# Sample gathers put ahead of the gate tables, and second-stage matmuls with activations as weights and 512 moving columns

## The chip, the cores and the metric

One core of one Trainium2 chip runs the whole step; the other cores are idle. The metric is device time in microseconds (us) of one execution. Below, PE is TensorE, DVE is VectorE, ACT is ScalarE, POOL is GpSimd, SP is the queue that issues the plain transfers.

## The reference

One layer of a hybrid decoder on two groups of tokens: a prompt of 512 tokens (four tiles of 128, with 16 learned tokens in front) and 32 sample tokens. The first half (projection, RWKV-7 recurrence, windowed attention, output projection) is not touched. The second half is the retrieval of experts:

```
h = rmsnorm(x, norm2_g)
q = h @ w_query;  s = q . sub_keys                  # 8 heads, two halves of 128 keys
idx, gate = top 16 of the sums of the top 16 of each half, softmax   # 128 experts per token
pre = einsum('td,tkd->tk', h, expert_u[idx])
act = gelu(pre) * gate
x   = x + einsum('tk,tkd->td', act, expert_v[idx]);   y = rmsnorm(x)
```

expert_u and expert_v have 16384 rows of 1024 numbers each (64 MB each).

## The kernel before, in words

The kernel serves the experts in two ways.

**By gathers** (prompt tiles 0 and 3, and the samples): `experts` fetches, for each of the k chosen experts, one row per token with an indirect transfer of 128 x 1024 numbers (512 KB), issued by POOL into one of six buffers `gat`. First all u rows (DVE multiplies each with h and sums it into a column of `pre`; the page calls this CUSTOM_DVE_ANT_0), then gelu and gate, then all v rows (DVE adds each, scaled, to the output `x`: SCALAR_TENSOR_TENSOR). A tile takes 128 + 128 gathers. The samples take 32 + 32, with the 32 tokens spread four times over the partitions, and end in three small transfers that fold the four parts, three adds and an rmsnorm.

**Densely** (prompt tiles 1 and 2, 256 tokens): all 16384 experts are computed for all tokens, in 128 blocks of 128 experts. `block_in` loads u and v of a block (one `uv` buffer, 1 MB), transposes u on PE, and splits u and v into two parts each whose sum is the value (uH, uL, vH, vL; the names ending in H and L are fp32r, TensorE's faster float format). ACT makes the H parts, DVE makes uL, POOL makes vL. `block_u` makes 24 matmuls of 256 columns, gelu on ACT, two multiplications by the gates and the split into aH, aL. `block_v` makes the second product and accumulates it over all 128 blocks in four PSUM banks `acc`.

The gates of the dense blocks are a table of experts by tokens. Function `gates`, run once for tile 1 and once for tile 2, builds it in 16 steps of 8 tokens each: a one-hot `o0` on DVE (written to a buffer called uH), a second one (buffer uL), six scalings on ACT, eight matmuls, copies out of PSUM. Between the steps run pieces of `late()`, the output projection and query scores of tile 3. The top-16 search of tile 3 (`late_heads`) runs beside the first dense blocks, and tile 3's gathers beside the others.

**What sets the order.** Gathers stand in a list `side` of generators. `beside(n)` takes n steps (one gather each) from the list and emits them at that place; `tc.issue_after(mark)` lets the scheduler put them as early as the marked DVE instruction. The scheduler then orders each engine's instructions by its own model of time; engines run their instructions in that order. Before the gates, `for n in range(AHEAD)` emits 280 steps: all of tile 0 and the first of the samples. Each of the 32 gate steps calls `beside(RATE_G)` with 0.8. Each dense block calls it with 1.6 while `late_heads` runs and with 2.4 afterwards. What is left comes at the end (`beside(1000)`).

The places to follow: the loop over AHEAD (L1619), `gates` with L1448, `block_v` (L1517 to L1524), the dense loop (L1645 to L1654) and the end (L1655 to L1671).

Of the kernel before, what the change touches and what calls it, by code (L numbers as in the profile page):

```python
# [11 lines left out]
F32 = mybir.dt.float32  # L12
# [3 lines left out]
OP = mybir.AluOpType  # L16
# [16 lines left out]
LAG = 2  # L33
WST = 3
UV = 5
AHEAD = 280
RATE_G = 0.8
RATE_D = 2.4
RATE_H = 1.6
LATE = 2  # L40
# [69 lines left out]
def bc(ap, shape):  # L110
    return ap.to_broadcast(shape)
# [3 lines left out]
def hymba_step(ctx, tc, x_prompt, x_sample, cache_k, cache_v, state_wkv, state_shift, meta, norm1_g, w_in, mu, w0,  # L115
# [3 lines left out]
    A, G, T, DM = nc.scalar, nc.gpsimd, nc.tensor, nc.sync  # L119
    marks = []  # L120
# [10 lines left out]
    V = V()  # L131
    uid = [0]

    def _t(pool, tag, bufs, shape, dt=F32):
        uid[0] += 1
        return pool.tile(list(shape), dt, tag=tag, name=f"{tag}_{uid[0]}", bufs=bufs)
# [30 lines left out]
    ident = p0.tile([128, 128], F32, name="ident")  # L167
# [77 lines left out]
    side, due = [], [0.0]  # L245

    def beside(n):

        due[0] += n
        while side and due[0] >= 1.0:  # L250
            due[0] -= 1.0
            if next(side[0], None) is None:
                side.pop(0)
        due[0] = min(due[0], 1.0)
# [845 lines left out]
    def finish(x2, y, rows, dst, gf, kind="F"):  # L1100

        rms(x2[:rows], y[:rows], rows, gf, kind)
        DM.dma_start(dst, y[:rows])

    def final_g(t):
        G.dma_start(t, fin_g.partition_broadcast(128))
        return t
# [96 lines left out]
    with ExitStack() as px:  # L1204
# [36 lines left out]
        def transposed(h, half, rows):  # L1241
            p = jps().rearrange("p (a b) -> p a b", a=4)
            for j in range(4):
                k = 4 * half + j
                transpose(p[:, j, 0:rows], h[:rows, k * 128:(k + 1) * 128])
            return p

        def put(src, dst):

            A.copy(dst[0], src)  # L1250
            V.tensor_tensor(dst[1], src, dst[0].bitcast(F32), OP.subtract)
# [25 lines left out]
        for half in range(2):  # L1277
            p = transposed(hS, half, 72)
# [144 lines left out]
    def gates(its, sel, ps, put):  # L1423


        i1T, i2T, gaT = sel
        its, iot = its
        ib = dt_("aH", 2, [128, 2, 128], BF16)
        for c, x in enumerate((i1T, i2T)):
            A.copy(ib[:, c], x)  # L1430
        for n, t8 in enumerate(range(0, 128, 8)):
            ob = dt_("uL", 2, [128, 128, GA], BF16)
            o0, o1 = dt_("uH", 2, [128, 8, 128]), dt_("vH", 2, [128, 8, 128])
            V.tensor_tensor(o0.rearrange("p t j -> p j t"), its, bc(ib[:, 0, t8:t8 + 8].unsqueeze(1), [128, 128, 8]), OP.is_equal)
            V.tensor_tensor(ob, its[:, :, 0:GA], bc(ib[:, 1, t8:t8 + GA].unsqueeze(1), [128, 128, GA]), OP.is_equal)
            for q0 in (0, 4):
                p = ps()
                for q in range(q0, q0 + 4):
                    t = slice(t8 + q, t8 + q + 1)
                    if q < GA:  # L1440
                        A.mul(o1[:, q, :], ob[:, :, q], gaT[:, t])
                    else:
                        V.tensor_scalar(o1[:, q, :], iot, i2T[:, t], gaT[:, t], OP.is_equal, OP.mult)
                    T.matmul(p[:, 128 * (q - q0):128 * (q - q0) + 128], o0[:, q, :], o1[:, q, :], start=True, stop=True)  # L1444
                put(t8 + q0, p)
            if n % LATE:
                next(more, None)
            with tc.issue_after(marks[-1]):  # L1448
                beside(RATE_G)


    ND = 256
    dn = ctx.enter_context(tc.tile_pool(name="dn", bufs=1, reuse_waits="tile"))
    dp = ctx.enter_context(tc.tile_pool(name="dp", bufs=1, space=PSUM, reuse_waits="tile"))

    def dt_(tag, bufs, shape, dt=F32):
        return _t(dn, tag, bufs, shape, dt)

    def dps():
        return _t(dp, "w", 4, [128, 512])  # L1460
# [3 lines left out]
    for i in range(2):  # L1464
        hn = dt_("uv", UV, [128, 2, D])[:, 0]
        DM.dma_start(hn, hscr[1 + i])
        for half in range(2):
            p = dps().rearrange("p (a b) -> p a b", a=4)
            for j in range(4):
                k = 4 * half + j  # L1470
                T.transpose(p[:, j, :], hn[:, 128 * k:128 * k + 128], ident)
            o = hH[:, 4 * half:4 * half + 4, 128 * i:128 * i + 128]
            A.copy(o, p)
            V.tensor_tensor(hL[:, 4 * half:4 * half + 4, 128 * i:128 * i + 128], p, o.bitcast(F32), OP.subtract)

    acc = [dp.tile([128, 2, ND], F32, name=f"acc{c}", bufs=1) for c in range(4)]
    euv = eu[0].rearrange("(i j) d -> i j d", j=128)
    evv = ev[0].rearrange("(i j) d -> i j d", j=128)

# [36 lines left out]

    def block_v(j, x):  # L1517
        vH, vL, aH, aL = x
        for d in range(8):
            o = acc[d // 2][:, d % 2, :]  # L1520
            ds_ = slice(128 * d, 128 * d + 128)
            T.matmul(o, vH[:, ds_], aH, start=(j == 0 and d % 2 == 0), stop=False, skip_group_check=True)  # L1522
            T.matmul(o, vH[:, ds_], aL, start=False, stop=False, skip_group_check=True)  # L1523
            T.matmul(o, vL[:, ds_], aH, start=False, stop=(j == 127), skip_group_check=True)  # L1524

    gA, gB = dt_("gA", 1, [128, 32, 128]), dn.tile([128, 64, 128], F32, name="gB")
    sg = [None]
# [88 lines left out]
            yield True  # L1616
        coming[0] = False

    for n in range(AHEAD):  # L1619
        with tc.issue_after(marks[gather_mark[0]]):  # L1620
            beside(1)
    more = late()
    its = one_hot_table()
    sels = [sel_transposed(0, dps, dt_("selT", 1, [128, 3, 128])), sel_transposed(1, dps, dt_("lsc", 1, [128, 3, 128]))]
    gates(its, sels[0], dps, stage)
    gates(its, sels[1], dps, keep)
    for _ in more:
        pass
# [15 lines left out]
    for j in range(128):  # L1644
        nxt, mark = None, last  # L1645
        if j < 127:
            nxt, last = block_u(ins.pop(j + 1), gate_of(j + 1))
        if j < 126:
            ins[j + 2], sub = block_in(j + 2)
        block_v(j, mid)  # L1650
        mid = nxt
        next(more, None)
        with tc.issue_after(mark), tc.issue_after(sub):
            beside(RATE_H if coming[0] else RATE_D)  # L1654
    oT = gB[:, 0:16, :].rearrange("p a b -> p (a b)").rearrange("p (a b) -> p a b", b=ND)  # L1655
    for c in range(4):
        A.copy(oT[:, 2 * c:2 * c + 2, :], acc[c])
    gfd = final_g(dt_("uv", UV, [128, 2, D])[:, 0])
    for i in range(2):
        xy = dt_("uv", UV, [128, 2, D])  # L1660
        x2, y = xy[:, 0], xy[:, 1]
        DM.dma_start(x2, xscr[1 + i])
        for half in range(2):
            p = dps()
            for q in range(4):
                k = 4 * half + q
                T.transpose(p[:, 128 * q:128 * q + 128], oT[:, k, 128 * i:128 * i + 128], ident)
            xs_ = x2[:, 512 * half:512 * half + 512]
            V.tensor_tensor(xs_, xs_, p, OP.add)
        finish(x2, y, 128, y_p[0, 128 * (i + 1):128 * (i + 1) + 128, :], gfd, "E")  # L1670
    beside(1000)  # L1671

# [27 lines left out]
```

## Time and profile before

| what | value |
|---|---|
| median of 3 runs | 2180.15 us (2161.02, 2180.15, 2190.67) |
| the profiled execution | 2171.7 us |
| its span, first to last instruction | 2169.9 us |
| mean granted TensorE clock | 0.866 of full speed |
| PE busy, DVE busy, POOL busy, ACT busy | 84%, 76%, 59%, 40% of the span |
| mean transfer rate | 263 GB/s |

All places in time below are us from the span's start. The busy shares are means over stages with different limits; what matters is read per stage. The gate tables begin at 1115.7 and end at 1247.2, the dense blocks run until about 2125.

### The profile page before, as it was taken

How to read it: one execution, taken by the hardware profiler on the slowest of the kernel's cores; microseconds unless marked ns; L12 is line 12 of the kernel's file. 1: busy time of each engine (PE TensorE's matmuls, PEld its weight loads, DVE VectorE, ACT ScalarE, POOL GpSimd, SP SyncE). 2: the span in 40 equal slices, each digit the busy share in tenths (PEclk: the TensorE clock that was granted, in tenths of full speed). 3: DMA queues.
4: the chain of work that ended last, by engine and by line, in shares of the span. 5: the costliest groups of instructions: out<-in, count | busy, mean ns of one | idle time of the engine just before them, and what ended most of it. 6: DMA issues, size and time to landing. Idle time of an engine off the chain costs nothing.

```text
span 2169.9 us, 37101 instructions
## 1 busy us (share of the span) xinstructions
PE 1816.4 (84%) x13915; PEld 1693.1 (78%) x13915; DVE 1639.2 (76%) x3285; ACT 862.6 (40%) x1975; POOL 1271.9 (59%) x951
## 2 busy tenths in 40 slices
PE   5999984585685868898567998999999999999992
PEld 5888973373574757798457988899999999999992
DVE  5643426679878988678989999867676767899988
ACT  6553421221132322433258943444444444444442
POOL 0110103678777677533824365768776777888885
PEclk9999986555675768799769999999999999999996
DMA  7532373487779789966859985789999998999987
GB/s 222 164 107 81 106 199 108 156 304 237 262 247 308 242 282 323 299 222 206 271 182 330 341 287 191 287 297 392 336 336 336 330 338 330 326 322 328 328 312 261
DMA packets 311306, 571.60 MB, mean 263 GB/s; under 512 B 32916, under 2 KB 194694, under 8 KB 310983
## 3 DMA queue, kind: packets, MB, share of 16 engines
q0 software_dynamic: 84048, 305.70, 39.6%
q1 hardware_dynamic: 227078, 263.53, 37.5%
q8 instruction: 110, 1.80, 0.3%
q14 instruction: 70, 0.57, 0.1%
HBM read 544.12 MB, written 25.65 MB: 263 GB/s over the span
## 4 chain that ended last, share of the span: by engine, by line
PE 56%; DVE 17%; issue 9%; DMA 8%; POOL 7%; ACT 3%; SPq 0%; POOLq 0%; DVEq 0%; ACTq 0%
PE acc L1523 5%; PE acc L1524 5%; PE acc L1522 5%; PE w L1508 5%; PE w L1505 5%; PE w L1506 5%; PE w L1491 4%; POOL gat L1075 4%; PE pD L220 3%; DVE x L127 3%; PE pD L966 2%; DVE gat L127 2%; DMA wst<-in_w_query_dram 2%; PE ps L220 2%; PE w L1444 2%
## 5 line engine op out<-in xcount | busy, mean ns | idle before, releaser
L127 DVE SCALAR_TENSOR_TENSOR x<-gat,act,x 128x1024 f32<-128x1024 f32 x287 | 440.5, 1535 | 12.5 <-DMA gat<-in_expert_v_dram,ei 9.4
L1075 POOL DMA_INDIRECT gat<-in_expert_u_dram,ei x256 | 337.0, 1316 | 132.2 <-DVE pre L127 45.8
L1075 POOL DMA_INDIRECT gat<-in_expert_v_dram,ei x256 | 317.7, 1241 | 122.6 <-issue 35.4
L1498 POOL TENSOR_TENSOR vL<-uv,vH 128x1024 fp32r<-128x1024 f32 x128 | 335.2, 2619 | 84.0 <-ACT vH L1497 82.7
L1522 PE MATMUL acc<-aH,vH 128*128 128x256 f32 x1024 | 292.2, 294 | 6.2 <-ACT aH L1514 6.2
L1523 PE MATMUL acc<-aL,vH 128*128 128x256 f32 x1024 | 289.5, 285 | 7.0 <-DVE aL L127 6.8
L1524 PE MATMUL acc<-aH,vL 128*128 128x256 f32 x1024 | 288.6, 284 | 0.0
L1505 PE MATMUL w<-dhH,uH 128*128 128x256 f32 x1024 | 251.6, 283 | 2.7 <-DVE uL L127 1.5
L1506 PE MATMUL w<-dhL,uH 128*128 128x256 f32 x1024 | 251.3, 283 | 0.0
L127 DVE CUSTOM_DVE_ANT_0 gat<-gat,h 128x1024 f32<-128x1024 f32 x160 | 202.7, 1279 | 44.7 <-DMA gat<-in_expert_u_dram,ei 41.7
L1523 PEld LDWEIGHTS acc<-aL,vH 128*128 128x128 f32 x1024 | 197.2, 193 | 8.9 <-DVE aL L127 8.8
L1505 PEld LDWEIGHTS w<-dhH,uH 128*128 128x128 f32 x1024 | 196.7, 192 | 3.1 <-DVE uL L127 1.7
L1522 PEld LDWEIGHTS acc<-aH,vH 128*128 128x128 f32 x1024 | 192.7, 192 | 7.1 <-ACT aH L1514 7.1
L1524 PEld LDWEIGHTS acc<-aH,vL 128*128 128x128 f32 x1024 | 197.1, 192 | 0.0
L1506 PEld LDWEIGHTS w<-dhL,uH 128*128 128x128 f32 x1024 | 196.7, 192 | 0.0
L1497 ACT CAST vH<-uv 128x1024 fp32r<-128x1024 f32 x128 | 134.9, 1054 | 148.9 <-issue 111.3
L127 DVE TENSOR_TENSOR uL<-w,uH 128x512 fp32r<-128x512 f32 x256 | 166.7, 682 | 10.1 <-ACT uH L1493 10.1
L127 DVE TENSOR_TENSOR w<-w,gl 128x128 f32<-128x128 f32 x128 | 50.3, 393 | 148.6 <-ACT w L1509 148.6
L127 DVE CUSTOM_DVE_ANT_0 gat<-gat,lx 128x1024 f32<-128x1024 f32 x128 | 158.1, 1268 | 0.0
L1508 PE MATMUL w<-dhH,uL 128*128 128x256 f32 x1024 | 148.1, 286 | 4.7 <-DVE uL L127 4.3
L1493 ACT CAST uH<-w 128x512 fp32r<-128x512 f32 x256 | 138.0, 593 | 8.0
L1508 PEld LDWEIGHTS w<-dhH,uL 128*128 128x128 f32 x1024 | 133.0, 192 | 7.6 <-DVE uL L127 6.9
(568 smaller groups left out, 4046.5 us busy)
## 6 DMA issues: line engine op xcount, KB each, us to landing
uv<-in_expert_u_dram SPq DMA_DIRECT2D x128, 512.0 KB, 4.5
uv<-in_expert_v_dram SPq DMA_DIRECT2D x128, 512.0 KB, 6.0
wst<-in_w_query_dram SPq DMA_DIRECT2D x48, 512.0 KB, 6.6
wst<-in_w_out_dram SPq DMA_DIRECT2D x24, 512.0 KB
wst<-in_w_in_dram SPq DMA_DIRECT2D x20, 512.0 KB, 4.4
h2T<-in_w_in_dram SPq DMA_DIRECT2D x20, 512.0 KB, 4.2
gscr<-uv SPq DMA_DIRECT2D x10, 1024.0 KB, 5.9
uv<-in_w_query_dram SPq DMA_DIRECT2D x8, 1024.0 KB, 12.2
```

The costliest lines, as they stand in the source:

```text
L127: r = getattr(nc.vector, name)(*args, **kw)
L220: T.matmul(p[:, 0:n], w[:, k, :], x, start=(k == 0 and x is H and w is wH), stop=(k == 7 and w is wL))
L1075: G.indirect_dma_start(out=r, out_offset=None, in_=w[0], in_offset=bass.IndirectOffsetOnAxis(ap=ei[:, k:k + 1], axis=0))
L1493: A.copy(uH[:, ks, :], p)
L1497: A.copy(vH, vn)
L1498: G.tensor_tensor(vL, vn, vH.bitcast(F32), OP.subtract)
L1505: T.matmul(pre, uH[:, k, :], hH[:, k, :], start=(k == 0), stop=False)
L1506: T.matmul(pre, uH[:, k, :], hL[:, k, :], start=False, stop=False)
L1508: T.matmul(pre, uL[:, k, :], hH[:, k, :], start=False, stop=(k == 7))
L1522: T.matmul(o, vH[:, ds_], aH, start=(j == 0 and d % 2 == 0), stop=False, skip_group_check=True)
L1523: T.matmul(o, vH[:, ds_], aL, start=False, stop=False, skip_group_check=True)
L1524: T.matmul(o, vL[:, ds_], aH, start=False, stop=(j == 127), skip_group_check=True)
```

## The change

Two edits.

The loop over AHEAD becomes `while side:`, so all gathers of tile 0 and all 64 of the samples, with the samples' final norm, are emitted before the gates. The call of `beside` inside `gates` goes. The dense loop is as it was; its `beside` finds an empty list until tile 3's gathers are appended.

`block_v` changes its operands. Before, each block of 128 columns of v was the weight and 256 token columns of a moved past it: 24 matmuls of 256 columns, with outputs of model dimension by token. Now a block of 128 tokens of a is the weight and 512 columns of v move past: 12 matmuls of 512 columns, with outputs of token by model dimension. The four PSUM banks are now plain 128 x 512, and at the end the copies to `oT` and 16 transposes go, since the sums already stand the right way round.

```diff
-AHEAD = 280
-RATE_G = 0.8
...
             if n % LATE:
                 next(more, None)
-            with tc.issue_after(marks[-1]):
-                beside(RATE_G)
...
-    acc = [dp.tile([128, 2, ND], F32, name=f"acc{c}", bufs=1) for c in range(4)]
+    acc = [dp.tile([128, 512], F32, name=f"acc{c}", bufs=1) for c in range(4)]
...
         vH, vL, aH, aL = x
-        for d in range(8):
-            o = acc[d // 2][:, d % 2, :]
-            ds_ = slice(128 * d, 128 * d + 128)
-            T.matmul(o, vH[:, ds_], aH, start=(j == 0 and d % 2 == 0), stop=False, skip_group_check=True)
-            T.matmul(o, vH[:, ds_], aL, start=False, stop=False, skip_group_check=True)
-            T.matmul(o, vL[:, ds_], aH, start=False, stop=(j == 127), skip_group_check=True)
+        for n, (a, v) in enumerate(((aH, vH), (aH, vL), (aL, vH))):
+            for i in range(2):
+                for c in range(2):
+                    T.matmul(acc[2 * i + c], a[:, 128 * i:128 * i + 128], v[:, 512 * c:512 * c + 512],
+                             start=(j == 0 and n == 0), stop=(j == 127 and n == 2))
...
-    for n in range(AHEAD):
+    while side:
         with tc.issue_after(marks[gather_mark[0]]):
             beside(1)
...
-    oT = gB[:, 0:16, :].rearrange("p a b -> p (a b)").rearrange("p (a b) -> p a b", b=ND)
-    for c in range(4):
-        A.copy(oT[:, 2 * c:2 * c + 2, :], acc[c])
...
-            p = dps()
-            for q in range(4):
-                k = 4 * half + q
-                T.transpose(p[:, 128 * q:128 * q + 128], oT[:, k, 128 * i:128 * i + 128], ident)
             xs_ = x2[:, 512 * half:512 * half + 512]
-            V.tensor_tensor(xs_, xs_, p, OP.add)
+            V.tensor_tensor(xs_, xs_, acc[2 * i + half], OP.add)
```

How this moves instructions, at three places. First DVE, from the end of tile 2's top-16 search (dsel, ce) over the preparation of the dense part (dhL) to the first one-hot of the gate tables (the first uH). Before:

```order
L127 TENSOR_REDUCE dsel_16_111<-ce_7163 128x32
L127 TENSOR_TENSOR ce_7167<-iota_87,hl_7152 128x512
L127 TENSOR_REDUCE dsel_17_112<-ce_7167 128x32
L127 TENSOR_TENSOR ce_7171<-iota_87,hl_7152 128x512
L127 TENSOR_REDUCE dsel_17_112<-ce_7171 128x32
L127 TENSOR_TENSOR dhL<-w_7873,dhH 128x4x128
L127 TENSOR_TENSOR dhL<-w_7896,dhH 128x4x128
L127 TENSOR_SCALAR vH_8792<-aL_8771,selT_8775 128x128 x2
L127 TENSOR_TENSOR uH_8791<-vL_8773,aH_8787 128x128x8
```

With the change (x_1953 is the samples' output, to which a v gather is added):

```order
L125 TENSOR_REDUCE dsel_16_111<-ce_7163 128x32
L125 SCALAR_TENSOR_TENSOR x_1953_8803<-gat_8829,act_8800,x_1953_8803 128x1024
L125 TENSOR_TENSOR ce_7167<-iota_87,hl_7152 128x512
L125 SCALAR_TENSOR_TENSOR x_1953_8803<-gat_8832,act_8800,x_1953_8803 128x1024
L125 SCALAR_TENSOR_TENSOR x_1953_8803<-gat_8835,act_8800,x_1953_8803 128x1024
L125 TENSOR_REDUCE dsel_17_112<-ce_7167 128x32
L125 SCALAR_TENSOR_TENSOR x_1953_8803<-gat_8838,act_8800,x_1953_8803 128x1024
L125 TENSOR_TENSOR ce_7171<-iota_87,hl_7152 128x512
L125 SCALAR_TENSOR_TENSOR x_1953_8803<-gat_8841,act_8800,x_1953_8803 128x1024
L125 TENSOR_TENSOR dhL<-w_7873,dhH 128x4x128
L125 SCALAR_TENSOR_TENSOR x_1953_8803<-gat_8865,act_8800,x_1953_8803 128x1024
L125 TENSOR_TENSOR uH_8949<-vL_8931,aH_8945 128x128x8
```

In all, 21 of the samples' 32 u gathers stood ahead of the first uH and 11 between the gate steps; all 32 stand ahead now. Of the 32 v gathers 14 stood between gate steps and 18 in the dense part; now 22 stand ahead of the first uH and 10 between the first six gate steps. The order of every engine up to the 21st u gather is unchanged.

Second POOL, at the beginning of the dense part (vL is the dense split, eis the samples' indices, leq of tile 3's search). Before:

```order
L1498 TENSOR_TENSOR vL_10394<-uv_10374,vH_10393 128x1024
L1075 DMA gat_10619<-in_expert_v_dram,eis_102 128x1024
L1075 DMA gat_10711<-in_expert_v_dram,eis_102 128x1024
L1498 TENSOR_TENSOR vL_10494<-uv_10474,vH_10493 128x1024
L1075 DMA gat_10714<-in_expert_v_dram,eis_102 128x1024
L1075 DMA gat_10811<-in_expert_v_dram,eis_102 128x1024
L1053 TENSOR_TENSOR leq_11000<-leq_11000,ld_2334_10910 128x512
L1498 TENSOR_TENSOR vL_10579<-uv_10559,vH_10578 128x1024
```

With the change:

```order
L1073 DMA gat_8895<-in_expert_v_dram,eis_102 128x1024
L1124 DMA gat_8903<-x_1953_8803 32x1024
L1104 DMA gat_8913<-in_final_norm_g_dram 128x1024
L1132 DMA x_3149_15637<-xscr 128x1024
L1494 TENSOR_TENSOR vL_10168<-uv_10148,vH_10167 128x1024
L1012 TENSOR_TENSOR lcand_10455<-lvals_10300 128x2x16 x2
L1494 TENSOR_TENSOR vL_10191<-uv_10171,vH_10190 128x1024
```

Twelve of the samples' gathers stood between the first ten vL; none does now. Tile 3's search is spread over the first 12 dense blocks where it was spread over 17, and its gathers are used from the same block on (the 15th), two per block in the mean, as before. After the last aL, DVE has 24 v gathers left where it had 22.

Third PE, one dense block. Before (24 such matmuls):

```order
L1491 MATMUL w_14718<-ident,uv_14706 128x128 x4
L1522 MATMUL acc_7903<-aH_14614,vH_14552 128x256
L1523 MATMUL acc_7903<-aL_14615,vH_14552 128x256
L1524 MATMUL acc_7903<-aH_14614,vL_14553 128x256
L1522 MATMUL acc_7904<-aH_14614,vH_14552 128x256
```

With the change (12 such matmuls; the order of u matmuls, transposes and v matmuls within a block is the same):

```order
L1487 MATMUL w_16728<-ident,uv_16716 128x128 x4
L1518 MATMUL acc_7903<-vH_16586,aH_16636 128x512
L1518 MATMUL acc_7904<-vH_16586,aH_16636 128x512
L1518 MATMUL acc_7903<-vL_16587,aH_16636 128x512
L1518 MATMUL acc_7903<-vH_16586,aL_16637 128x512
```

## Rows read from the trace of the kernel before

**Rows 1.** The page: busy time of each engine.

```profile
PE 1816.4 (84%) x13915; PEld 1693.1 (78%) x13915; DVE 1639.2 (76%) x3285; ACT 862.6 (40%) x1975; POOL 1271.9 (59%) x951
```

**Rows 2.** Busy time of each engine by stretch; columns are named in the first line.

```profile
core 0: us, PE busy (x) PEld busy (x) DVE busy (x) ACT busy (x) POOL busy (x), PEclk, DMA share, GB/s
1021.10:1084.80 63.70, 34.94 (x253) 31.75 (x251) 60.03 (x183) 15.63 (x46) 54.13 (x52) 0.83 0.87 275
1084.80:1115.70 30.90, 15.82 (x62) 11.92 (x62) 25.57 (x122) 9.71 (x26) 9.89 (x15) 0.50 0.67 212
1115.70:1176.80 61.10, 44.27 (x283) 41.16 (x283) 54.74 (x87) 50.22 (x127) 22.11 (x12) 0.87 0.81 266
1176.80:1247.20 70.40, 69.86 (x594) 67.59 (x593) 65.85 (x84) 66.86 (x238) 26.70 (x14) 1.00 0.96 332
1255.00:1400.40 145.40, 130.57 (x1034) 126.21 (x1033) 141.08 (x356) 60.41 (x111) 91.18 (x72) 0.96 0.70 246
1400.40:1884.00 483.60, 483.60 (x4093) 483.60 (x4092) 341.63 (x637) 205.17 (x367) 358.65 (x224) 1.00 0.91 337
1884.00:2118.00 234.00, 233.56 (x1960) 232.46 (x1959) 216.78 (x250) 96.68 (x175) 199.86 (x111) 1.00 0.91 320
2118.00:2169.90 51.90, 9.25 (x63) 8.51 (x61) 41.67 (x39) 12.07 (x31) 27.84 (x23) 0.63 0.74 264
```

**Rows 3.** The chain that ended last, 1087 to 1109: start, us, what.

```profile
1087.65 2.09 DVE idxu L127 x8
...
1107.33 1.28 POOL ce L1053
```

**Rows 4.** Timeline of POOL: first and 27th of the samples' u gathers.

```profile
1021.16 1.03 POOL L1075 DMA_INDIRECT gat<-in_expert_u_dram,eis  x1 [1.61 <-DVE eis L127]
...
1087.09 0.98 POOL L1075 DMA_INDIRECT gat<-in_expert_u_dram,eis  x1 [0.16 <-DVE sD L127]
```

**Rows 5.** DVE's groups, 1021 to 1084.8: count, busy and mean ns, idle before.

```profile
L127 DVE CUSTOM_DVE_ANT_0 gat<-gat,h 128x1024 f32<-128x1024 f32 x21 | 31.7, 1515 | 2.7 <-DMA gat<-in_expert_u_dram,eis 2.7
```

**Rows 6.** DVE's groups in the gate tables, 1115.7 to 1247.2.

```profile
L127 DVE SCALAR_TENSOR_TENSOR x<-gat,act,x 128x1024 f32<-128x1024 f32 x13 | 16.7, 1281 | 0.0
L127 DVE CUSTOM_DVE_ANT_0 gat<-gat,h 128x1024 f32<-128x1024 f32 x11 | 13.3, 1214 | 0.0
...
L127 DVE TENSOR_TENSOR act<-act,gas 128x32 f32<-128x32 f32 x1 | 0.2, 191 | 2.2 <-ACT act L1089 2.2
```

**Rows 7.** DVE's groups in the first dense blocks, 1255 to 1400.4.

```profile
L127 DVE SCALAR_TENSOR_TENSOR x<-gat,act,x 128x1024 f32<-128x1024 f32 x18 | 35.3, 1964 | 0.0
...
L127 DVE CUSTOM_DVE_ANT_0 gat<-gat,lx 128x1024 f32<-128x1024 f32 x7 | 11.7, 1705 | 0.0
...
L127 DVE TENSOR_TENSOR h<-h,gat 32x1024 f32<-32x1024 f32 x3 | 4.8, 1584 | 0.4 <-DMA gat<-x 0.4
```

**Rows 8.** Timeline of ACT: gelu of the 1st, 20th and 21st dense block.

```profile
1254.96 0.37 ACT L1509 ACTIVATE w<-w 128x256 f32<-128x256 f32 x1 [2.48 <-PE w L1508]
...
1400.43 0.37 ACT L1509 ACTIVATE w<-w 128x256 f32<-128x256 f32 x1 [1.91 <-PE w L1508]
...
1407.05 0.37 ACT L1509 ACTIVATE w<-w 128x256 f32<-128x256 f32 x1 [1.91 <-PE w L1508]
```

**Rows 9.** Timeline of PE: merged runs, start, us to the last one's end, count.

```profile
252.77 3.67 PE L220 MATMUL pD<-gat,wst 128*128 128x314 f32 x24
...
1125.99 3.62 PE L1574 MATMUL w<-uv,ly 128*128 128x256 f32 x16
...
1606.45 0.28 PE L1523 MATMUL acc<-aL,vH 128*128 128x256 f32 x1
...
1609.08 0.28 PE L1524 MATMUL acc<-aH,vL 128*128 128x256 f32 x1
```

**Rows 10.** Timeline of DVE within a late dense block: two v gathers of tile 3.

```profile
1935.68 4.61 DVE L127 SCALAR_TENSOR_TENSOR x<-gat,act,x 128x1024 f32<-128x1024 f32 x2
```

**Rows 11.** DVE's groups at the end, 2125 to 2165.

```profile
L127 DVE SCALAR_TENSOR_TENSOR x<-gat,act,x 128x1024 f32<-128x1024 f32 x23 | 29.5, 1283 | 2.5 <-DMA gat<-in_expert_v_dram,ei 2.1
```

## The prediction, put on record before the changed kernel was timed

> **What bounds the kernel now.** I read the page's busy times first [rows 1]: no engine fills the span, PE is nearest. So the question is put to stages, with the table of busy time by stretch [rows 2], and there the limit changes three times. From 1021.1 to 1084.8 DVE is busy 60.0 of 63.7 us, and in the next 30.9 us 25.6; the chain there runs along DVE and, in short handshakes, POOL [rows 3]. In the gate tables (1115.7 to 1247.2) DVE has 120.6 of 131.5 us, ACT 117.1, PE 114.1: all three nearly full, PE fullest in the second half (69.9 of 70.4). In the first dense blocks (1255 to 1400.4) DVE is full (141.1 of 145.4) and PE is not (130.6). From 1400.4 to 1884 PE has no idle time at all and DVE 71%; one block takes 1407.05 - 1400.43 = 6.62 us, by the gelus [rows 8]. From 1884 on DVE is at 93% beside a full PE, and the last 51.9 us belong to leftover gathers on DVE, with PE nearly done.
>
> So the moved gathers leave two stretches that are full on several engines for one that is full on DVE alone, and the shorter matmul stream pays only where PE sets the pace.
>
> **The sum**, against the profiled execution's own 2171.7 us.
>
> 1. *The front, +42 us.* The order is unchanged up to the 21st u gather, about 1084.8. From there to the first one-hot, 33 gathers are new on DVE: 11 u and 22 v. Nearest prices: 1.21 us for a u gather and 1.28 for a v gather in the gates [rows 6], 1.28 for v at the end [rows 11], 1.52 for u in the stretch just before [rows 5]. At 11 x 1.21 + 22 x 1.28 they are 42 us, at 1.52 each they are 50. Idle DVE time to fill is 30.9 - 25.6 = 5.3 us [rows 2], handshakes with POOL of the kind that the chain shows [rows 3]. So 37 at the least, 45 at the most by DVE's work; I take 42. Transfers agree: 33 x 0.52 MB is 17 MB, with the 6.5 MB that the stretch moves now 24 MB, which at the 332 GB/s of the second gate half [rows 2] is 72 us, against 30.9 + 42 = 73. The issues on POOL have room (9.9 us busy of 30.9). The upper end is the pace seen just before: 27 gathers issued in 1087.09 - 1021.16 us [rows 4], 2.54 us each with the other work of that stretch in it; 33 x 2.54 = 84, which is +53 over the 30.9. Nothing else runs that could cover this: PE is at half clock (0.50) and half idle there already, so its clock loses nothing more either.
>
> 2. *The gates, -3 us.* DVE loses 11 u and 14 v gathers, and the 2.2 us wait on the samples' gelu [rows 6], and gets 10 v gathers and the samples' three adds and norm, all in the first six steps: about 33 us off, 17 on. But the first steps stay at DVE's pace, and the second half is at PE's. At best the stage falls to ACT's 117 us, that is -14; at worst the ten gathers lengthen the first steps by as much as the rest gains, 0.
>
> 3. *The first 19 dense blocks, -14 us.* They take 145.4 us, 19.6 more than 19 x 6.62. DVE's 18 v gathers of the samples took 35.3 us there (1.96 each, slowed), the three adds of the fold 4.8 [rows 7]; without them DVE has 101 us of work, and on POOL twelve gathers no longer stand between the vL splits. Against this, tile 3's search is packed into 12 blocks where it had 17. Its DVE work: a block's own is 341.6 / 73 - 2 x 1.21 = 2.3 us by the steady stretch [rows 2, 6], 43 in 19 blocks; with 11.7 for tile 3's first gathers [rows 7] some 46 of the 101 are search. In 12 blocks that is 46 + 12 x 2.3 = 73 us against 12 x 6.5 = 78: nearly full, with handshakes besides. I leave 8 us of the excess and count the shorter matmuls (19 x 0.13). Bounds: -5 (DVE still sets all 12 blocks) and -22.
>
> 4. *The 512-column matmul, -9 us, where PE sets the pace.* No fp32r matmul of 512 columns is in the trace. At 256 columns the step from one to the next is (1609.08 - 1606.45) / 22 = 119.5 ns; at 314 columns (3.67 - 0.31) / 23 = 146.1 ns [rows 9], where 0.31 is the duration of the last one. Per column that is 0.467 and 0.465 ns: by proportion 512 columns take 239 ns and nothing is won. The other end is a stream of 512 array cycles with the smallest overhead in the trace: the plain-float matmuls of 256 columns, at two cycles a column of the 2.4 GHz clock, follow each other at (3.62 - 0.38) / 15 = 216 ns [rows 9]. The two fp32r points lie about 13 and 15 ns over columns / 2.4 GHz, so I take a cost per matmul of 13 to 15 ns, and 228 ns. A block then takes 12 x 228 = 2.74 us for its v part, where it took 24 x 119.5 = 2.87: 0.13 us less. From 1400.4 to 1884, with PE never idle, there are 73 blocks: -9. At the bounds 0 and 73 x 0.28 = -20.
>
> The Trainium skill speaks against a gain: its page "TensorE: Matmul & The Clock Gate", section "LDWEIGHTS (loading the stationary operand)", has a load cost columns / 1.2 ns, 107 ns for 128 columns, which a 256-column stream already covers, so that halving the number of loads frees nothing. The page's "Back-to-back issue gap" has the isolated step at N / 2.4 + 2.5 ns, an estimate of 109 ns at 256 columns and 216 at 512; the trace has 119.5 at 256, so it does not hold here as it stands. By it the term would be as in the first rival below.
>
> 5. *The last 35 blocks, -2 us.* Two v gathers take 4.61 us of DVE in such a block, slowed from 1.28 each [rows 6, 10], and DVE is at 93% over the whole stretch [rows 2]: 6.49 us is less than DVE's work in many of these blocks. Bounds 0 and 35 x 0.13 = -5.
>
> 6. *The end, +2 us.* It is bound by the gathers: 24 instead of 22 after the last aL, 2 x 1.28 [rows 11]. The four copies on ACT and 16 transposes on PE that go were beside these gathers, so they give nothing; were the gathers not there, they would give 2 to 3 us.
>
> Sum: 42 - 3 - 14 - 9 - 2 + 2 = +16, that is 2171.7 + 16 = 2188 us. The profiled execution is 8 us below the median of the three runs, 2180.15, so against the median this is +0.4%. Two per cent, about what a measurement of this kernel can tell from no change, is 43.6 us: 2136.5 to 2223.8.
>
> **Rivals.**
>
> *Thin overhead.* The 512-column matmul steps at 216 ns. For: the 256-column plain-float row [rows 9] shows a step that close to its stream. Against: both fp32r points are 13 to 15 ns over theirs. Terms 3 and 4 gain another 2 and 11 us: 2175. Chance 0.17. This is the time that the page's issue-gap rule would give as well.
>
> *The front runs at the gathers' old pace (slower).* The front stretches by 53 because each gather goes through issue, transfer, DVE and the release of one of six buffers at 2.54 us [rows 4], while the search's handshakes hold POOL. For: that is the pace measured in the stretch just before, with POOL busy 54 of 63.7 us [rows 2]. Against: DVE was the full engine there and waited only 2.7 us for a transfer [rows 5], and it had (60.0 - 31.7) / 21 = 1.35 us of other work per gather, against 25.6 / 33 = 0.78 now. 2171.7 + 53 - 26 = 2199. It is slower by over 2% once the front grows by 78, that is from a pace of (78 + 30.9) / 33 = 3.3 us on; if the gathers lay wholly behind the search at 2.54, +84, the time would be 2230. Chance 0.21, of which 0.08 for more than 78.
>
> *DVE was the only brake.* The gates fall to ACT's 117 us and the first blocks to PE's, 42 - 14 - 22 - 9 - 2 + 2 = -3: 2169. For: DVE is the busiest engine in both. Against: in the second gate half PE is at 99%. Chance 0.15.
>
> *The change does not move what it says.* Excluded: the new order shows the gathers moved and 12 matmuls per block.
>
> **How the numbers follow.** The forecast has 0.45, the rivals 0.17, 0.21 and 0.15, and 0.02 is left for none of these. The likeliest case gives 2188. The range goes from the two favourable rivals together, 2169 - 13 = 2156, to the pace rival and half the spread of the runs shown above it (2199 + 15), with a few us more on each side for what varies between runs: 2152 to 2220. The favourable rivals together still stand 20 us above 2136.5, so faster by over 2%: 0.05. Slower by over 2%: 0.08 from the pace rival and 0.03 of chance in the runs, 0.11. Within 2%: 0.84.
>
> **What would show each step.** Front: the first uH about 42 us after 1115.7, near 1158, with DVE busy all the way and PE nearly idle. Gates: 125 to 130 us from first uH to last gate matmul. First dense blocks: gelu 1 to gelu 20 in about 131 us. PE: steps of 226 to 231 ns between the acc matmuls, blocks of 6.49 us. Last blocks: DVE nearly full, blocks still near 6.6. End: about 54 us from the last gelu. I am wrong on the main term if the first uH comes before 1148 or after 1170, and on the matmul if the step is under 220 or over 236 ns.

## The result, and the profile after

The changed kernel takes 2192.5 us (median of 20 runs, 2180.8 to 2200.1), the kernel before 2168.2 (20 runs, 2159.2 to 2190.7). The ratio is 1.0104, with a 95% interval of 1.0086 to 1.0121: slower by 1%, within two per cent. The forecast was 2188 us, +0.7% on its own profiled execution.

The page after, and its busy time by stretch (columns as in [rows 2]):

```profile
PE 1812.6 (83%) x12363; PEld 1628.4 (74%) x12363; DVE 1676.1 (76%) x3285; ACT 862.5 (39%) x1972; POOL 1276.0 (58%) x951
```

```profile
1080.90:1149.50 68.60, 15.55 (x62) 12.06 (x62) 65.23 (x168) 13.71 (x31) 56.95 (x48) 0.50 0.93 328
1149.50:1180.00 30.50, 22.19 (x121) 20.63 (x122) 30.43 (x38) 18.56 (x47) 11.15 (x8) 0.74 0.85 257
1180.00:1227.40 47.40, 34.90 (x227) 32.95 (x227) 35.37 (x50) 38.12 (x99) 1.49 (x3) 0.82 0.70 209
1227.40:1290.80 63.40, 62.85 (x530) 60.54 (x530) 44.73 (x62) 60.32 (x221) 0.00 (x0) 1.00 0.69 229
1302.30:1425.60 123.30, 120.58 (x818) 110.90 (x818) 94.12 (x293) 57.42 (x102) 69.29 (x54) 1.00 0.60 218
1425.60:1901.50 475.90, 475.79 (x3214) 438.81 (x3213) 386.49 (x635) 203.71 (x366) 378.50 (x222) 1.00 0.93 338
1901.50:2133.60 232.10, 231.01 (x1541) 211.30 (x1540) 221.91 (x249) 97.44 (x175) 197.39 (x108) 1.00 0.90 320
2133.60:2191.00 57.40, 7.89 (x24) 5.64 (x23) 44.87 (x42) 9.73 (x27) 31.60 (x26) 0.57 0.76 265
```

The page hardly moved: PE lost 3.8 us of busy time, DVE gained 36.9. The stretches moved a lot. In the front DVE is busy 65.2 of 68.6 us with PE at half clock and mostly idle; the second gate half lost 14.8 us of DVE work and did not get a microsecond shorter, since PE fills it (its row before stands next); the first dense blocks are now PE's.

```profile
1183.90:1247.20 63.30, 62.76 (x530) 60.49 (x530) 59.49 (x75) 60.25 (x221) 24.35 (x13) 1.00 0.97 336
```

To place the microseconds I use marks that both traces have: the first sample gather on POOL [rows 4], the first one-hot uH, the 17th (the first of tile 2), the last gate matmul, and the 1st, 20th and last gelu [rows 8]. After, by the timelines of POOL, DVE and ACT:

```profile
1018.00 1.04 POOL L1073 DMA_INDIRECT gat<-in_expert_u_dram,eis  x1 [1.62 <-DVE eis L125]
```

```profile
1149.54 3.62 DVE L125 TENSOR_TENSOR uH<-vL,aH 128x1024 f32<-128x1024 bf16 x2
```

```profile
1302.33 0.37 ACT L1505 ACTIVATE w<-w 128x256 f32<-128x256 f32 x1 [4.18 <-PE w L1504]
...
1425.60 0.37 ACT L1505 ACTIVATE w<-w 128x256 f32<-128x256 f32 x1 [1.78 <-PE w L1504]
...
1432.09 0.37 ACT L1505 ACTIVATE w<-w 128x256 f32<-128x256 f32 x1 [1.78 <-PE w L1504]
...
2133.63 0.37 ACT L1505 ACTIVATE w<-w 128x256 f32<-128x256 f32 x1 [0.35 <-PE w L1504]
```

The first sample gather itself, ahead of everything that was changed, came anywhere from 1012.6 to 1032.1 us in the traces of this study, so the stretches are counted from it. For every kernel of the study (us):

| kernel | front | gates 1 | gates 2 | to 1st gelu | first 19 blocks | other blocks | end | sum |
|---|---|---|---|---|---|---|---|---|
| before | 94.6 | 68.2 | 63.3 | 7.8 | 145.5 | 717.6 | 51.8 | 1148.7 |
| the change | 131.5 | 77.9 | 63.3 | 11.6 | 123.3 | 708.0 | 57.4 | 1173.0 |
| gathers_only | 130.5 | 76.7 | 63.2 | 10.7 | 125.8 | 718.0 | 52.1 | 1177.0 |
| block_v_only | 94.3 | 70.3 | 63.4 | 7.8 | 144.9 | 708.0 | 58.4 | 1147.1 |
| narrow_256 | 130.5 | 77.5 | 63.3 | 11.3 | 124.7 | 716.1 | 53.5 | 1176.9 |
| bv_rate270 | 97.2 | 70.4 | 63.5 | 7.8 | 145.1 | 711.4 | 57.1 | 1152.4 |
| late_fold | 131.2 | 72.3 | 63.2 | 11.5 | 126.2 | 708.3 | 57.5 | 1170.3 |
| spread_v | 127.7 | 65.7 | 63.4 | 10.5 | 126.2 | 708.3 | 56.2 | 1158.1 |
| bv_gates130 | 95.7 | 75.8 | 68.9 | 6.5 | 126.3 | 708.0 | 56.5 | 1137.8 |
| bv_a292 | 106.3 | 72.4 | 62.8 | 18.0 | 122.9 | 708.0 | 58.1 | 1148.4 |
| bv_a292_late | 105.9 | 70.1 | 63.2 | 7.8 | 126.9 | 708.0 | 57.4 | 1139.3 |
| cut_before | 94.1 | 68.2 | 63.4 | 7.8 | 145.4 | 718.5 | 20.4 | 1117.8 |
| cut_block_v | 93.6 | 70.6 | 63.3 | 7.8 | 145.1 | 708.8 | 18.2 | 1107.4 |

The change by this table: front +36.9, gates +9.7, way to the first gelu +3.8, first blocks -22.2, other blocks -9.6, end +5.6, together +24.3. One of the twelve executions of bv_a292 took 4269 us, about twice the others, and its ratio below leaves it out.

### The profile page after: what moved, and what is told of

Same layout as the page of the kernel before. It is cut to its first block, busy times and chain, and to the rows that moved or that the text cites. A ratio compares the mean times of both kernels' runs of the same rounds, so it can differ in the third digit from the quotient of the medians.

```text
span 2191.0 us, 33999 instructions
## 1 busy us (share of the span) xinstructions
PE 1812.6 (83%) x12363; PEld 1628.4 (74%) x12363; DVE 1676.1 (76%) x3285; ACT 862.5 (39%) x1972; POOL 1276.0 (58%) x951
## 4 chain that ended last, share of the span: by engine, by line
PE 50%; DVE 22%; issue 10%; POOL 7%; DMA 7%; ACT 4%; SPq 0%; POOLq 0%; DVEq 0%; ACTq 0%
PE acc L1518 11%; DVE x L125 5%; POOL gat L1073 4%; PE w L1504 4%; DVE gat L125 4%; PE w L1501 4%; PE w L1502 4%; PE w L1487 4%; PE pD L218 3%; PE pD L964 2%; DVE uL L125 2%; PE ps L218 2%; DMA wst<-in_w_query_dram 2%; PE w L1442 2%; PE pB L503 1%
## 5 line engine op out<-in xcount | busy, mean ns | idle before, releaser
L1494 POOL TENSOR_TENSOR vL<-uv,vH 128x1024 fp32r<-128x1024 f32 x128 | 342.2, 2673 | 159.7 <-ACT vH L1493 157.0
L125 DVE CUSTOM_DVE_ANT_0 gat<-gat,lx 128x1024 f32<-128x1024 f32 x128 | 194.4, 1553 | 0.0
L1518 PE MATMUL acc<-vH,aH 128*128 128x512 f32 x512 | 151.3, 415 | 4.3 <-ACT aH L1510 4.3
L1518 PE MATMUL acc<-vL,aH 128*128 128x512 f32 x512 | 139.1, 393 | 0.0
L1518 PE MATMUL acc<-vH,aL 128*128 128x512 f32 x512 | 137.5, 390 | 0.0
L1487 PE MATMUL w<-ident,uv 128*128 128x128 f32 x1024 | 133.6, 273 | 0.9 <-ACT uv L1540 0.9
L125 DVE TENSOR_TENSOR w<-w,gl 128x128 f32<-128x128 f32 x128 | 50.7, 396 | 106.5 <-ACT w L1505 106.3
L964 PE MATMUL pD<-h2T,wst 128*128 128x128 f32 (+1 forms) x768 | 114.8, 307 | 15.9 <-DMA wst<-in_w_query_dram 15.1
L1510 ACT CAST aH<-w 128x256 fp32r<-128x256 f32 x128 | 48.5, 379 | 189.9 <-DVE w L125 189.8
```

The lines of the kernel that those rows point to most:

```text
L125: r = getattr(nc.vector, name)(*args, **kw)
L964: T.matmul(p[:, 0:tot], wt[:, k, :], h2T[:, k, :], start=(k == 0), stop=(k == 7))
L1487: T.transpose(p[:, q, :], un[:, 128 * k:128 * k + 128], ident)
L1494: G.tensor_tensor(vL, vn, vH.bitcast(F32), OP.subtract)
L1518: T.matmul(acc[2 * i + c], a[:, 128 * i:128 * i + 128], v[:, 512 * c:512 * c + 512], start=(j == 0 and n == 0), stop=(j == 127 and n == 2))
```

## The experiments

**The two parts apart.** gathers_only takes the kernel before and moves the gathers alone; block_v_only leaves them and changes the second stage alone.

```diff
 # gathers_only, from the kernel before
-    for n in range(AHEAD):
+    while side:
...
-            with tc.issue_after(marks[-1]):
-                beside(RATE_G)
```

> The gathers' part alone, with the matmuls as before. Theory (the two parts add up, and the gathers explain all of the front, the gates and the first blocks): front +34, gates +10, way to the first gelu +4, first 19 blocks -20 (the shorter matmuls' 19 x 0.13 missing), steady blocks 0 at 6.62 us each, end +3 to +5: +31 us on the kernel before, ratio 1.013 to 1.016. Rival (the operand change is worth nothing and the steady blocks got shorter because the samples' gathers left them): +21, ratio 1.010, blocks of 6.49 us here too.

Measured: 2199.0 us, ratio 1.0121 (1.0097 to 1.0144), blocks of 6.62 us. By the table +28.3, a little under the theory's +31; the rival's 6.49 us blocks are not there. All of the loss is the gathers'.

> The new second stage alone, gathers where they were before. Theory: blocks of 6.49 us from the 20th gelu on, nothing in the first 19 blocks because DVE sets their pace: -9 to -13 us, ratio 0.994 to 0.996; acc step 228.6 ns. Rival (the last third is at DVE's and the transfers' pace, and a shorter block meets them at once): 0 to -5 us, ratio 0.998 to 1.000. Rival (first blocks gain too): -13 to -17, ratio 0.992.

Measured: 2165.4 us, ratio 0.9986 (0.9958 to 1.0014). The blocks are 6.49 us and the dense part is 9.6 us shorter, as the theory has it, but the total is only 1.6 us (trace) to 3 us (ratio) less, as the first rival has it, and the interval contains 1. The reason is mostly not that rival's: the end is 6.6 us longer and the first gate half 2.1. The leftover gathers on POOL after the last gelu, of before, of the change and of this kernel:

```profile
L1075 POOL DMA_INDIRECT gat<-in_expert_v_dram,ei x21 | 25.6, 1217 | 9.4 <-issue 4.4 <-DVE x L127 3.8 <-DVE sE L127 0.9
```

```profile
L1073 POOL DMA_INDIRECT gat<-in_expert_v_dram,ei x24 | 28.7, 1195 | 11.2 <-DVE x L125 5.9 <-issue 5.3
```

```profile
L1075 POOL DMA_INDIRECT gat<-in_expert_v_dram,ei x24 | 29.8, 1241 | 11.1 <-DVE x L127 5.8 <-issue 5.0 <-DMA gat<-in_expert_v_dram,ei 0.3
```

A gather takes (25.6 + 9.4) / 21 = 1.67 us there with its waits. How many issues fall behind the last gelu (21 or 24) hangs on a microsecond; on DVE the count is firmer. Behind the last gelu it has 27 v adds of tile 3 in every kernel with the 512-column stage whose gathers are not cut, and 25 with 256 columns (24 and 22 behind the last aL): two more. From add to add it is 1.65 us before, 1.73 in the change and 1.77 in block_v_only. For block_v_only that makes 3.5 us for two adds and 2.5 for the slower pace, and the adds begin 0.7 later: the 6.6. Why the pace is slower is not shown. Much of what PE saves inside the blocks comes back behind them. gathers_only, with the old blocks, has an end of 52.1.

**Number of matmuls or role of operands.** narrow_256 is the change with 256 columns of v moving, 24 matmuls a block.

```diff
-                for c in range(2):
-                    T.matmul(acc[2 * i + c], a[...], v[:, 512 * c:512 * c + 512], ...)
+                for c in range(4):
+                    T.matmul(acc[2 * i + c // 2][...], a[...], v[:, 256 * c:256 * c + 256], ...)
```

> The change with activations as weights, but 24 matmuls of 256 moving columns in place of 12 of 512. Theory (a fixed cost of 13 to 15 ns for each matmul, whatever moves): step 119.5 ns, block 6.62 us, about +31 us on the kernel before, ratio 1.013 to 1.016, like the gathers' part alone. Rival (the role of the operands makes it, the number of weight loads or their source does not): step about 114 ns, block 6.49, +21, ratio 1.010.

Measured: 2200.2 us, ratio 1.0139 (1.0114 to 1.0164), blocks of 6.62 us. The second stage of one block, first of the change, then of narrow_256 (start, us to the end of the last one, count):

```profile
1608.02 1.17 PE L1518 MATMUL acc<-vH,aH 128*128 128x512 f32 x4
1609.02 1.08 PE L1518 MATMUL acc<-vL,aH 128*128 128x512 f32 x4
1609.94 1.07 PE L1518 MATMUL acc<-vH,aL 128*128 128x512 f32 x4
1610.85 0.28 PE L1501 MATMUL w<-dhH,uH 128*128 128x256 f32 x1
```

```profile
1702.46 1.12 PE L1518 MATMUL acc<-vL,aH 128*128 128x256 f32 x8
1703.42 1.12 PE L1518 MATMUL acc<-vH,aL 128*128 128x256 f32 x8
```

At 512 columns four take 1609.94 - 1609.02 = 0.92 us, 230 ns each, and the next four 0.91, 228 ns (the first four, which follow the transposes, 1.00); at 256 columns eight take 0.96, 120 ns each, as with the old operands [rows 9]. So the role of the operands is worth nothing; the count is, (2 x 120 - 229) = 11 ns for each matmul that goes, 12 x 11 = 0.13 us a block. Each matmul has a weight load of its own in all three kernels, so whether the 11 ns belong to the matmul or to its load is not shown.

**Does the end take the gain back?** Two kernels in which tile 3 uses 96 of its 128 experts a token, so that no gathers are left after the blocks: the kernel before, and block_v_only.

```diff
-                side.append(tile_experts(3, *pl1, held[0]))
+                side.append(tile_experts(3, *pl1, held[0], nk=96))
```

> The kernel before with tile 3's gathers cut from 128 to 96 experts a token (64 gathers and their DVE work left out), so that the gathers end before the dense blocks do. Both theories: no adds after the last block, the last gelu about where it was or up to 9 us earlier, the way from the last gelu to the end 51.8 to about 20 us: ratio 0.980 to 0.986 to the kernel before. It is the base of the next kernel.

Measured: 2135.7 us, ratio 0.9875 (0.9844 to 0.9907); the end is 20.4 us.

> The same cut with the new second stage. Theory (the shorter blocks gain 10 us, and 6 to 7 of it go back after the last block, because the leftover gathers run at the transfers' pace of 1.7 us and three more of them are left): with no gathers left over the gain stays, 108 x 0.13 = 14 us in the blocks and 2 to 3 for the copies and transposes at the end: -14 to -17 us on the cut kernel before, 0.7%. Rival (the stage gains only about 3 us wherever it stands, since first blocks or transfers take the rest): -2 to -5 us on it.

Measured: 2125.9 us, ratio 0.9799 (0.9774 to 0.9825). Between the two it is -9.8 us by the medians and -10.4 by the traces (-0.76% by the ratios, whose intervals are 0.3% each way). The end is now 2.2 us shorter with the new stage, where with the leftovers it was 6.6 longer: that half of the theory holds, and the 2 to 3 us for copies and transposes with it. The total lies between the theory's 14 to 17 and the rival's 2 to 5, since the blocks gain 9.7 us, not 14: of the 108 blocks 27 stand more than 0.06 us above 6.49, 11 us in all, where 6 stood so above 6.62, 6 us in all. Why is not shown. The first gate half is 2.4 us longer, with no edit there (70.3 to 70.6 in the three kernels with the new stage and the old rates before the blocks, 68.2 in the two with the old). The scheduler put the samples' u dots at other places between the one-hots; that these make the 2.4 us was not tried.

**More gathers in each block.** bv_rate270 is block_v_only with `RATE_D = 2.7` for 2.4.

> The new second stage alone, with 2.7 instead of 2.4 gathers a block after the search of tile 3. Theory (PE sets the pace of the dense blocks, and what is left over at the end is 22 gathers that had no place): no gathers left after the last block, the end falls from 52 to about 27 us, the blocks stay at 6.49: ratio 0.982 to 0.986. Rival (transfers at 337 GB/s and DVE at 93% are full in the dense blocks, so that what leaves the end lengthens the blocks): end shorter by 25, dense part longer by 15 to 30, ratio 0.992 to 0.998.

Measured: 2171.4 us, ratio 1.0006 (0.9984 to 1.0029): the end stays at 57.1 us, and the other blocks take 3.4 us more. Neither was right as put: the rate is not what limits. The engines' order has mostly two gathers a block from about the 48th block on at either rate (the 48th gather of tile 3 stands in block 38 and the 192nd in block 108 with both), so the extra steps never reached the blocks. What held the scheduler to two is open.

**Why the gates grew.** In the first gate half after the change, DVE has ten v adds of the samples in the first six steps (this timeline begins with the fourth step and its five adds), then the samples' norm:

```profile
1162.96 1.95 DVE L125 TENSOR_TENSOR uH<-vL,aH 128x1024 f32<-128x1024 bf16 x1
1164.76 0.57 DVE L125 TENSOR_SCALAR vH<-aL,selT 128x128 f32<-128x128 f32 x2
1165.26 1.27 DVE L125 SCALAR_TENSOR_TENSOR x<-gat,act,x 128x1024 f32<-128x1024 f32 x1
1166.46 0.54 DVE L125 TENSOR_TENSOR uL<-vL,aH 128x768 bf16<-128x768 bf16 x1
1166.93 2.58 DVE L125 SCALAR_TENSOR_TENSOR x<-gat,act,x 128x1024 f32<-128x1024 f32 x2
1169.43 0.41 DVE L125 TENSOR_TENSOR lx<-lx,w 128x256 f32<-128x256 f32 x1
1169.76 2.60 DVE L125 SCALAR_TENSOR_TENSOR x<-gat,act,x 128x1024 f32<-128x1024 f32 x2
1172.28 1.94 DVE L125 TENSOR_TENSOR uH<-vL,aH 128x1024 f32<-128x1024 bf16 x1
...
1212.25 1.27 DVE L125 SCALAR_TENSOR_TENSOR gat<-h,sF,gat 32x1024 f32<-32x1024 f32 x1 [0.18 <-ACT sF L202]
1213.45 1.27 DVE L125 SCALAR_TENSOR_TENSOR lx<-lx,sE,uv 128x1024 f32<-128x1024 f32 x1
1220.20 1.97 DVE L125 TENSOR_TENSOR uH<-vL,aH 128x1024 f32<-128x1024 bf16 x1 [5.48 <-PE w L1442]
```

The next one-hot comes 9.3 us after the last, where this step took 4.3 before and the steps from the third to the tenth 3.4 to 4.7. Later the 32-row norm of the samples runs on ACT and DVE interleaved with tile 3's own, right ahead of it, and PE waits for tile 3's:

```profile
1214.77 1.54 PE L182 MATMUL w<-ident,lx 128*128 128x128 f32 x6 [8.13 <-DVE lx L125]
```

This wait alone proves little: it is 7.4 us in the kernel before and 8.1 in block_v_only, which have no samples' norm there. The step around it, the 14th, takes 13.5 us in the change, 9.4 before and 11.5 in block_v_only.

late_fold keeps all gathers ahead and sends the last two adds, the fold and the norm to the first dense block; spread_v puts 53 sample gathers ahead and spreads the last 11 over the 32 gate steps.

```diff
 # late_fold, from the change
-    while side:
+    for n in range(321):
 # spread_v, from block_v_only (late fold too)
-AHEAD = 280
-RATE_G = 0.8
+AHEAD = 310
+RATE_G = 0.35
```

> The change, but the samples' last two adds, the fold and the final norm are emitted after the gates, with the first dense block; all 64 gathers stay ahead. Theory (the first gate half grew from 68.2 to 77.9 us in two places: about 5 us where ten v adds stand between one-hots on DVE, about 4 us where the samples' norm stands on ACT and DVE ahead of tile 3's norm): the second part goes, first half 73 to 74 us, first 19 blocks 2 to 4 us longer for the three adds of 1.2 us and the norm; in all 0 to -4 us on the change. Rival (the v adds alone make it, the norm is beside other work): first half 77 to 78 us. Rival (neither; the one-hots merely meet tile 3's output projection at another place): 76 to 80 us with the wait of 8 us on DVE still there.

Measured: 2187.6 us, ratio 1.0092 (1.0066 to 1.0117). First half 72.3, the first blocks 2.9 us longer, -2.7 us by the table: near the theory's numbers. The total alone would not show it, since its interval overlaps that of the change. But the 5.6 us are not won where the theory saw them. The 14th step falls only from 13.5 to 12.5, with PE's wait at 7.1; the rest goes in five earlier steps, at 0.6 to 1.3 us each, among them the two that lost an add. So the two adds, the fold and the norm cost 5.6 us there mainly as work between the one-hots; the place ahead of tile 3's norm accounts for about 1.

> The change with 53 sample gathers ahead and the last 11, all of v, spread over the 32 gate steps (0.35 for each step), fold and norm with the first dense block. Theory (ten v adds packed into the first six gate steps hold up the one-hots of step 5, and the samples' norm does the rest): front 131 as with the change, first gate half 66 to 70 instead of 77.9 us, second half 63 to 64.5: -6 to -11 us on the change, ratio to the kernel before 1.005 to 1.008. Rival (a gather costs the same on DVE wherever it stands in the gates): first half 72 as with the late fold alone, second half 66 to 68, ratio 1.009 to 1.011.

Measured: 2177.5 us, ratio 1.0061 (1.0034 to 1.0087). First half 65.7, even under the 68.2 of before, second half 63.4 with its v adds in it at no cost. By the table it is -14.9 us on the change, more than the theory's 6 to 11: the front is 3.8 shorter as well, with three v adds fewer in it. Since only five adds are left in the first half, spread_v does not separate the packing from the number. bv_a292_late below does: it has 14 v adds in the first half, never more than one to a step, and takes 70.1 us, where late_fold takes 72.3 with eight, all in the first four steps (the fold stands later in both). So the packing is shown, and the work of the fold and norm; what else lengthens the 14th step is open.

**Gathers where they cost least.** Two kernels on block_v_only: 1.3 sample gathers for each gate step; and 12 more ahead with 0.95 a step.

```diff
-RATE_G = 0.8        # bv_gates130
+RATE_G = 1.3
-AHEAD = 280         # bv_a292 (bv_a292_late: RATE_G = 0.92)
-RATE_G = 0.8
+AHEAD = 292
+RATE_G = 0.95
```

> The new second stage with the gathers where they were before the change, except 1.3 instead of 0.8 sample gathers for each gate step, so that all 64 are out by the end of the gates. Theory (gathers cost least where PE sets the pace, in the second gate half): front as before, first gate half 68 to 76 us, second half 63 to 68, first 19 blocks 123 to 128 us instead of 145: -8 to -18 us on the kernel before, ratio 0.992 to 0.996. Rival (the gates are at DVE's and the transfers' limit, 336 GB/s there before: each gather added costs 1.56 us): gates +25, nothing won, ratio 0.999 to 1.003.

Measured: 2157.9 us, ratio 0.9944 (0.9915 to 0.9973). The gates took 75.8 + 68.9 us, DVE 68.4 busy of 68.9 in the second half and transfers 347 GB/s: 16 more gathers there than in block_v_only cost 11 us, 0.7 each, between theory and rival; the first blocks gave back 18.6, and the total is in the theory's range.

> The same with 12 more gathers ahead of the gates and 0.95 for each gate step. Theory (1.05 us for a gather in the front, little in the gates): front +12, gates +3 to +6, first 19 blocks -20, matmuls -3 net: -2 to -8 us on the kernel before, ratio 0.996 to 0.999. Rival (gates at the limit of the transfers): +5, ratio 1.002.

Measured: 2167.7 us, ratio 0.9995 (0.9966 to 1.0024). Front, gates and blocks about as the theory has them, but 18.0 us from the last gate matmul to the first gelu. DVE's timeline there:

```profile
1274.21 1.21 DVE L127 TENSOR_TENSOR h<-h,x 32x1024 f32<-32x1024 f32 x1
...
1278.77 3.53 DVE L127 TENSOR_TENSOR h<-h,gat 32x1024 f32<-32x1024 f32 x1 [2.31 <-DMA gat<-x]
...
1283.28 1.86 DVE L127 TENSOR_TENSOR uL<-w,uH 128x512 fp32r<-128x512 f32 x3
1285.08 1.20 DVE L127 TENSOR_TENSOR h<-h,gat 32x1024 f32<-32x1024 f32 x1
```

The first add of the fold that needs a transferred part waits 2.3 us for it and then takes 3.5, and uL, which the first block's matmuls need, stands behind it. These matmuls begin 5.9 us later than in block_v_only; then the first gelu comes after 7.5 us instead of 3.2, with the last piece of uL behind another add and a granted clock of 0.68 instead of 1.00.

> As the kernel with 12 more gathers ahead, but 0.92 in place of 0.95 for each gate step, so that the samples' last two adds, fold and norm come with the first dense block. Theory (the 18 us between the last gate matmul and the first gelu there were the fold's adds, which stand ahead of the first block's uL on DVE and wait for a transfer of the folded part): that way falls to 7 to 9 us, the first 19 blocks gain 2 us of work, and the whole is 7 to 10 us shorter: ratio 0.994 to 0.997. Rival (it was tile 3's search, or the loads of the first block): 15 us or more there, ratio 0.999 to 1.000.

Measured: 2156.4 us, ratio 0.9942 (0.9921 to 0.9964); 7.8 us to the first gelu: one gather step fewer in the gates sends the fold behind uL. This and bv_gates130 are 0.6% under the kernel before, and so under the change as well.

## Why the prediction was right, and where its steps were not

The sign and the total came out (2188 forecast, 2192.5 measured), but part of the nearness is luck. The sum of the terms was +16, and by the table it was +24.3; the forecast stood on an execution 3.5 us above the median of the kernel before, which hides some of that. Of the terms, the gates, the way to the first gelu, the end and the later blocks came out 21.5 us too slow together, the front and the first blocks 13.3 too fast.

1. **Front, +42: measured +36.9**, the lower bound. The work was priced rightly: 11 u dots of 1214 ns and v adds of 1361 ns.

```profile
L125 DVE SCALAR_TENSOR_TENSOR x<-gat,act,x 128x1024 f32<-128x1024 f32 x21 | 28.6, 1361 | 1.1 <-DMA gat<-in_expert_v_dram,eis 0.8
L125 DVE CUSTOM_DVE_ANT_0 gat<-gat,h 128x1024 f32<-128x1024 f32 x11 | 13.3, 1214 | 0.0
```

With the first v gather, a multiplication of 0.7 us, that is 42.6 us by the durations. But instructions that follow each other overlap a little in the records (the next one starts 0.07 us before an add's end in the timeline above): DVE's busy time from the first gather to the first uH, which counts overlaps once, rose by 39.3 us, from 85.6 to 124.9. Its idle time there fell from 9.0 to 6.6; I had named 5.3 [rows 2] and counted on none of it. The pace rival (2.54 us a gather) fell: DVE waited 1.1 us in all for these adds. The transfers are nearly as full in this stretch, at 328 GB/s and a share of 0.93 in the table of stretches; that they would not have set the pace with a faster DVE is not shown.

2. **Gates, -3: measured +9.7**, outside the bounds of -14 to 0. This is the step that failed. That "at worst the ten gathers lengthen the first steps by as much as the rest gains" took DVE's total for the stage; the second half has no use for DVE's time (63.3 us with 59.5 or 44.7 busy), so nothing gained there could pay for the first. late_fold, spread_v and bv_a292_late show most of the growth: adds packed between one-hots, and 5.6 us for the last two adds, fold and norm.

3. **The way to the first gelu: not in the sum, measured +3.8.** Tile 3's search waits for its scores on DVE, in front of uL; before, uL was ahead of it. That starts the first u matmuls 1.5 us later. The other 2.3 us are the clock: PE, which had waited 3.0 us for uL, has a granted clock of 0.52 from there to the gelu, mostly its lower level of 1.2 GHz, and needs 5.5 us where it needed 3.2 at 1.00.

```profile
1292.67 0.87 DVE L125 MAX8 lvals<-lsc 128x8 f32<-128x128 f32 x4 [4.92 <-DMA lsc<-lscr]
...
1296.12 0.67 DVE L125 TENSOR_TENSOR uL<-w,uH 128x512 fp32r<-128x512 f32 x1
```

4. **First 19 blocks, -14: measured -22.2**, the other bound. The 8 us left for the packed search were not needed: 123.3 us is 19 x 6.49, with DVE at 94.1. The reason, v adds and fold out of DVE's way, holds: gathers_only gives -19.7 with the old matmuls.

5. **Matmul, -9 and -2: measured -9.6**, -7.7 in the first 73 of these blocks and -1.9 in the last 35. Step 228 to 230 ns for 228, block 6.49 for 6.49. Thin overhead (216 ns) fell. The Trainium skill, page "TensorE: Matmul & The Clock Gate", section "Back-to-back issue gap", has N / 2.4 + 2.5 ns for the isolated step at the full clock, an estimate of 216 at 512 columns; these rows have 228 to 230, and the measurement decides. The Trainium skill's section "LDWEIGHTS (loading the stationary operand)" on that page has the load cost alone; that halving the loads frees nothing was my conclusion from it. 11 ns went with each matmul and its load, and the two were not tried apart.

6. **End, +2: measured +5.6.** Two gathers more was right (24 adds for 22 behind the last aL). The price was not: from add to add it is 1.65 us before and 1.73 after, not DVE's 1.28, so DVE does not set their pace. In the POOL rows most of it is POOL's own issuing, the rest mainly waits for a buffer that a DVE add must free; transfers run at 328 GB/s there (2142 to 2174), so which of the two ends first is not settled.

DVE as the only brake was half right, for the first blocks; in the gates it is PE's second half that bounds them from below.

## What to carry to other kernels

Price a moved piece of work by the stage that it leaves and by the stage that it enters, half by half: a gather cost about 1.1 us in the front ((131.5 - 94.6) / 33), nothing in the second gate half, 0.7 where the gates were filled up, and 1.7 after the last block. When a stream that hides something gets shorter, look at what it hid: of the 9.6 us that PE saved in block_v_only, 6.6 came back behind the last block. And look at what stands first in each in-order queue where stages meet; with the fold's adds ahead of uL a whole stage came 10 us later, and one step of a count moved them away.

## What the runs showed of the hardware

An fp32r matmul of 512 columns steps at 228 to 230 ns, and one of 256 at 120, whichever operand is the weight. Plain-float matmuls of 256 columns step at 216 ns [rows 9]. Where PE had waited 3 us ahead of the first dense block, the granted clock was 0.52 of full, and a way of 3.2 us took 5.5. The time before the first sample gather varied by 19.5 us between profiled executions, though no edit touches it, against some 8 us for the width of the change's 95% interval; so parts are compared from a common mark, and totals by many runs.
